# Attention parts at fixed places of each product pair, and the silus in another order, in a float32 encoder block on one core

## The chip, the cores and the metric

The kernel runs on one core of one Trainium2 chip. The metric is the device time of one execution in microseconds (us). Times of several runs are given by their median. One further execution was taken with the hardware profiler; durations of single instructions come from it. TensorE (PE) does the matrix products, VectorE (DVE) and ScalarE (ACT) the elementwise work, GpSimd (POOL) and SyncE (SP) issue most of the DMAs.

## The reference

One layer over 1024 tokens of width 1024 in float32, cut to what matters here:

```python
h = rmsnorm(x, norm_g)
q, k, v, za, u, vs, zs, gm = split(h @ w_in)
a   = window_sink_attention(rope(q), rope(k), v, sinks)     # 16 heads, 2 key heads, chunks of 64, window 192
a   = (a * silu(za)) @ w_att_out
sgo = chunked_spatial_gating(gelu(u), gelu(vs), ...)        # result s1 in the kernel
sgo = (sgo * silu(zs)) @ w_sg_out
ga, gs = split(sigmoid(gm + b_merge))
y   = ga * a + gs * sgo
out = rmsnorm(x + y @ w_o, final_g)
```

The attention subtracts the row's maximum (or the sink, if that is larger), takes exp, adds exp of the sink to the sum, and divides.

## The kernel before, in words

Every large product is done for a pair of 128-row blocks of the result at once, by a seven-product scheme of Strassen's kind on halves of the operands. Each factor is split into a rounded part (h) and a rest (l), and each of the seven products is 12 matmuls of 128 x 512. `gemm_pair` (L347) runs them in the order b11, t1, t2, b21, t3, b22, t4, named after the form of the activations that they use. They gather in three PSUM tiles: `acc` in a bank of ps_mm (b11, t2, t3, t4), `t5` in one of ps_o (t1, b22) and `t2` in one of ps_o (b21). There are two banks of each name. ACT copies x11, x22 and x12 out behind b11, t1 and t2 (L356, L360, L363), DVE adds the rest behind b21, t3 and b22 (L368, L373, L377). Each finished quarter (i, half) is handed to `finish`, in the order (0,0), (1,1), (0,1), (1,0); the last comes straight from `acc`, with sign -1. Behind each product `gemm_pair` calls a `hook`, so there are seven hooks in a pair, and `split_next` (L205) splits weights of the next pair there (L152, L153).

The stretch that the change touches has twelve pairs. Four compute zs: `zs_pair` with m = 0, 2, 4, 6. Then come four that compute the gate gs and four that compute ga; these only store their quarters. In this text they are called Z0 to Z3, S0 to S3 and A0 to A3. `zs_pair` (L1014) keeps the four quarters until the pair's products are written, then has a silu for each (L1032) and a multiplication by a block of s1 (L1042), and stores the product. The blocks of s1 are fetched into tiles "rot" in Z0 (five buffers, shared with the rotation of queries) and "g" in Z1 to Z3 (two buffers; two fetches are issued at the third hook, the others when a buffer is free). `after` ties instructions of one engine to an order without a semaphore: the first silu comes behind the last exp that stands ahead of it in the program, and the other silus behind the first. Silu and Exp need different tables of ACT, which are loaded on each change.

The attention has 32 steps n, each a group of heads on 128 tokens, and is written as a generator, `attention` (L1173), that yields after each part. A step has three parts:

- s(n), `softmax_stage` (L1060): scores into the two banks of ps_sc (L1075), row minima on DVE (L1083, L1084), four exps on ACT (L1086), one for the sink (L1096), sum and reciprocal on DVE (L1097, L1099), scaling on DVE (L1105) and ACT (L1107). It is followed by the query loads of step n + 2 on SP (L1000).
- w(n), `weight_stage` (L1110): eight transposes into two banks of ps_tp (L1127, L1138), split on ACT and DVE (L152, L153, tiles pT and pTb).
- v(n), `value_stage` (L1143): six matmuls into a bank of ps_o (L1160), copied by ACT (L1166) and added by DVE (L1167) into aT; every second one stores aT on POOL (L1169) and has the next value loads issued on SP (L981 to L991).

The generator's order is s0, s1, w0, s2, and then w(n-2), s(n), v(n-3) over and over: 96 parts. `part_of_attention` (L1213) is the hook of Z1 to A3 and decides how many parts run at a hook: one at each in Z1, Z2 and Z3, and 75/56 on average in the other eight pairs, by a running credit. Seven and 75/7 do not divide by three, so each pair finds the cycle at another place. From Z2 on each hook also calls `part_of_early` (L436), which at every second call has POOL issue one step of sums of later weights.

What is written first has priority, but the order of an engine's instructions in the trace is not that of the program: the framework's scheduler fills an engine with what its own model holds to be ready.

Of the kernel before, what the change touches and what calls it, by code (L numbers as in the profile page):

```python
# [33 lines left out]
KC = D // P  # L34
# [18 lines left out]
def hybrid_tile(  # L53
# [101 lines left out]
    def after(second, first):  # L155

        tc.add_manual_dep(
            second.ins,
            first.ins.name,
            mybir.DependencyInfo(mybir.DependencyClass.NoSync, mybir.DependencyReason.DATA),  # L160
            reason="order",
        )
# [184 lines left out]
    def gemm_pair(b, finish, hook=lambda: None, second="o"):  # L347

        n = done[0]
        done[0] += 1
        acc = bank("mm")[:]
        x11, x12, x22 = xtile(), xtile(), xtile()
        product(acc, ready[n, 0], b["b11"], True)
        pace[0] = nc.scalar.copy(x11[:], acc)  # L356
        hook()
        t5 = bank("o")[:]
        product(t5, ready[n, 2], b["t1"], True)
        pace[0] = nc.scalar.mul(x22[:], t5, -1.0)  # L360
        hook()
        product(acc, ready[n, 3], b["t2"], False)
        pace[0] = nc.scalar.copy(x12[:], acc)  # L363
        split_next()
        hook()
        t2 = bank(second)[:]
        product(t2, ready[n, 1], b["b21"], True)
        term[0] = nc.vector.tensor_add(x11[:], x11[:], t2)  # L368
        finish(0, 0, x11, x11[:], 1.0)
        split_next()  # L370
        hook()
        product(acc, ready[n, 4], b["t3"], False)
        term[0] = nc.vector.tensor_sub(x22[:], x22[:], acc)  # L373
        finish(1, 1, x22, x22[:], 1.0)
        hook()
        product(t5, ready[n, 5], b["b22"], False)
        term[0] = nc.vector.tensor_add(x12[:], x12[:], t5)  # L377
        finish(0, 1, x12, x12[:], 1.0)
        split_next()
        hook()  # L380
        product(acc, ready[n, 6], b["t4"], False)
        finish(1, 0, xtile(), acc, -1.0)
        split_next()
        hook()
# [51 lines left out]
    def part_of_early(every=2):  # L436
        hooks[0] += 1
        if early and hooks[0] % every == 0:
            early.pop(0)()
# [4 lines left out]
    def put(dst, m, half, src, queue=nc.sync):  # L444
        queue.dma_start(place(dst, m, half), src)

    def get(src, m, half, bufs, tag="g"):
        g = mtile([P, HALF], F32, tag, bufs, pool)
        copy_to(g[:], place(src, m, half))
        return g  # L450
# [319 lines left out]
    def hook():  # L770
        for _ in range(2):
            if late:
                late.pop(0)()
# [240 lines left out]
    def zs_pair(m, hook, *place, ahead_by=0):  # L1014
        quarters, fetched, hooked = [], [], [0]

        def fetch(i, half):
            fetched.append(get(s1_dr, m + i, half, *place))

        def step():  # L1020
            hook()
            hooked[0] += 1
            if hooked[0] == ahead_by:
                for at in ((1, 0), (0, 0)):
                    fetch(*at)

        gemm_pair(hb, lambda *quarter: quarters.append(quarter), step)

        quarters = quarters[-1:] + quarters[:-1]
        first = None  # L1030
        for i, half, q, src, sign in quarters:
            silu = nc.scalar.activation(q[:], src, AF.Silu, scale=sign)  # L1032
            first = first or silu
            if silu is not first:
                after(silu, first)
            elif exps:
                after(silu, exps[-1])
        for i, half, q, src, sign in quarters:
            if not fetched:
                fetch(i, half)  # L1040
            g = fetched.pop(0)
            nc.vector.tensor_mul(q[:], q[:], g[:])  # L1042
            put(s_dr, m + i, half, q[:])

    steps_of_q += [rotate(1, 1), first_loads()]
    zs_pair(0, part_of_q, 5, "rot")
    stage.close()

# [124 lines left out]
    def attention():  # L1173

        held, weights = [], []
        tiles = [step[:2] for step in steps[::2]]

        def weigh(n):  # L1180
            weights.append(weight_stage(*steps[n], held.pop(0)))

        def value(n):
            value_stage(*steps[n], weights.pop(0))
            if n % 2 and n + 3 < len(steps):
                value_loads(*tiles[n // 2 + 2])

        for n, step in enumerate(steps):
            if n >= 2:
                weigh(n - 2)  # L1190
                yield
            held.append(softmax_stage(*step, qT.pop(0)))
            if n + 2 < len(steps):
                qT.append(query_stage(*steps[n + 2]))
            if n in (0, 2):
                value_loads(*tiles[n // 2])
            yield
            if n >= 3:
                value(n - 3)
                yield  # L1200
        last = len(steps)
        for n in (last - 2, last - 1):
            weigh(n)
            yield
            value(n - 1)
            yield
        value(last - 1)
        yield

    parts = attention()  # L1210
    credit = [0.0]

    def part_of_attention(m=KC):  # L1213
        if m > 2:
            part_of_early()
        credit[0] += 1 if m < KC else 75 / 56
        while credit[0] >= 1:
            credit[0] -= 1
            next(parts, None)

    for m in range(2, KC, 2):
        zs_pair(m, lambda: part_of_attention(m), 2, ahead_by=3)
    for dst in (gs_dr, ga_dr):
        for m in range(0, KC, 2):
            gemm_pair(hb, rest(dst, m), part_of_attention)
# [438 lines left out]
```

## Time and profile before

| | |
|---|---|
| median of 3 runs | 939.69 us (939.38, 939.69, 942.12) |
| profiled execution, its own time | 939.98 us |
| span from its first to its last instruction | 938.1 us |
| mean granted clock of TensorE | 0.996 |
| Z1 to A3, about | 322 to 622 us of the span |

A page of the profile gives the busy time and instructions of each engine, then groups of instructions, with what ended the idle time ahead of them ("<-"). L338 is the one line that issues the matmuls of all seven products; the tile names tell them apart. In the timeline a row is `start, duration, engine, line, operation, out<-in, shapes, count [idle before <-releaser]`. A matmul's duration is modelled and overlaps the next one, so the distance of starts is the better measure. The table by windows has the busy time of PE, PEld (weight loads), DVE, ACT and POOL in each stretch, then granted clock, DMA share and GB/s. The waits are listed as waiting line, releasing line: us in total, times, longest.

### The profile page before, as it was taken

The numbers are of one execution on the slowest core, as the hardware profiler recorded it, in microseconds if no ns is written. First come the engines' busy times: TensorE is split into PE (matmuls) and PEld (weight loads), VectorE is DVE, ScalarE is ACT, GpSimd is POOL, SyncE is SP. The second block draws the span as 40 slices with busy tenths as digits, with TensorE's granted clock in tenths as the row PEclk, the third lists the DMA queues.
The fourth block names the chain that finished last, engine by engine and source line by source line (L and its number), as shares of the span: only waits on it lengthen the run. The fifth ranks groups of instructions, "written<-read, shape, count | busy, mean of one in ns | idle before, by whom it ended". The sixth has DMA issues, their size and how long they took to land.

```text
span 938.1 us, 13590 instructions
## 1 busy us (share of the span) xinstructions
PE 917.9 (98%) x4525; PEld 768.9 (82%) x4525; DVE 677.0 (72%) x1218; ACT 531.6 (57%) x1057; POOL 123.0 (13%) x199
## 2 busy tenths in 40 slices
PE   7999999999999999999999999999999999999996
PEld 6898888888888878888888888888887887888885
DVE  6755577665668678787878877756499489668996
ACT  7864343333445468777656676744475565457443
POOL 1211212221000001111111111101110011210012
PEclk9999999999999999999999999999999999999999
DMA  7343767888686778777777778859668754998622
GB/s 282 120 149 119 216 212 200 173 164 178 214 271 232 244 217 212 214 201 206 202 209 249 236 177 239 229 178 379 209 203 308 282 197 157 294 298 297 203 112 114
DMA packets 131301, 201.60 MB, mean 215 GB/s; under 512 B 12320, under 2 KB 64032, under 8 KB 131232
## 3 DMA queue, kind: packets, MB, share of 16 engines
q1 hardware_dynamic: 113616, 152.23, 49.0%
q0 software_dynamic: 17472, 48.24, 21.3%
q8 instruction: 36, 0.59, 0.3%
q14 instruction: 33, 0.27, 0.1%
q10 hardware_dynamic: 144, 0.26, 0.1%
HBM read 144.59 MB, written 85.46 MB: 245 GB/s over the span
## 4 chain that ended last, share of the span: by engine, by line
PE 75%; DVE 11%; ACT 5%; DMA 4%; issue 4%; SPq 1%; DVEq 0%; ACTq 0%
PE ps_mm L338 29%; PE ps_o L338 22%; PE ps_mm L624 6%; PE ps_tp L338 2%; PE ps_o L575 2%; PE ps_sc L1075 2%; PE ps_o L1160 2%; PE ps_sc L338 2%; DVE wl L153 2%; PE ps_tp L818 2%; ACT pr L1086 1%; DVE bq L182 1%; PE ps_tp L624 1%; PE ps_sc L624 1%; PE ps_o L624 1%
## 5 line engine op out<-in xcount | busy, mean ns | idle before, releaser
L152 ACT CAST wh<-s 128x1024 fp32r<-128x1024 f32 (+1 forms) x76 | 76.0, 1003 | 92.1 <-PE ps_mm L338 43.9
L153 DVE TENSOR_TENSOR wl<-wr,wh 128x1024 fp32r<-128x1024 f32 (+1 forms) x78 | 73.7, 947 | 53.6 <-ACT wh L152 52.9
L152 ACT CAST wh<-wr 128x1024 fp32r<-128x1024 f32 (+1 forms) x78 | 64.4, 829 | 80.4 <-PE ps_mm L338 33.7
L153 DVE TENSOR_TENSOR wl<-s,wh 128x1024 fp32r<-128x1024 f32 (+1 forms) x76 | 88.5, 1165 | 17.8 <-ACT wh L152 16.2
L1086 ACT ACTIVATE pr<-ps_sc,sm 128x192 f32<-128x192 f32 (+2 forms) x128 | 51.1, 410 | 35.6 <-DVE sm L1084 27.8
L338 PE MATMUL ps_o<-T_t1h,wh 128*128 128x512 f32 x144 | 57.1, 397 | 0.3 <-ACT wh L152 0.2
L338 PE MATMUL ps_o<-T_b22h,wh 128*128 128x512 f32 x144 | 57.2, 397 | 0.0
L338 PE MATMUL ps_o<-T_t1h,wl 128*128 128x512 f32 x144 | 56.3, 391 | 0.1
L338 PE MATMUL ps_o<-T_b22h,wl 128*128 128x512 f32 x144 | 56.2, 390 | 0.0
L338 PE MATMUL ps_o<-T_b22l,wh 128*128 128x512 f32 x144 | 56.1, 390 | 0.0
L338 PE MATMUL ps_o<-T_t1l,wh 128*128 128x512 f32 x144 | 56.1, 390 | 0.0
L338 PE MATMUL ps_mm<-T_b11h,wl 128*128 128x512 f32 x136 | 53.3, 392 | 2.0 <-DVE wl L153 2.0
L338 PE MATMUL ps_mm<-T_t3h,wh 128*128 128x512 f32 x136 | 54.1, 398 | 0.0
L338 PE MATMUL ps_mm<-T_t4h,wh 128*128 128x512 f32 x136 | 53.9, 396 | 0.0
L338 PE MATMUL ps_mm<-T_b11h,wh 128*128 128x512 f32 x136 | 53.7, 395 | 0.0
L338 PE MATMUL ps_mm<-T_t2h,wh 128*128 128x512 f32 x136 | 53.3, 392 | 0.2 <-ACT x L356 0.2
L338 PE MATMUL ps_mm<-T_t3l,wh 128*128 128x512 f32 x136 | 53.2, 391 | 0.0
L338 PE MATMUL ps_mm<-T_t3h,wl 128*128 128x512 f32 x136 | 53.2, 391 | 0.0
L338 PE MATMUL ps_mm<-T_t4h,wl 128*128 128x512 f32 x136 | 53.2, 391 | 0.0
L338 PE MATMUL ps_mm<-T_t2h,wl 128*128 128x512 f32 x136 | 53.0, 390 | 0.0
L338 PE MATMUL ps_mm<-T_b11l,wh 128*128 128x512 f32 x136 | 53.0, 390 | 0.0
L338 PE MATMUL ps_mm<-T_t4l,wh 128*128 128x512 f32 x136 | 53.0, 390 | 0.0
(374 smaller groups left out, 2474.8 us busy)
## 6 DMA issues: line engine op xcount, KB each, us to landing
wr<-in_w_dram SPq DMA_DIRECT2D x82, 256.0 KB
sums<-in_w_dram POOLq DMA_DIRECT2D x20, 512.0 KB, 5.3
s<-sums SPq DMA_DIRECT2D x20, 512.0 KB
s_dr<-x SPq DMA_DIRECT2D x32, 256.0 KB
q_hl<-qhl SPq DMA_DIRECT2D x16, 512.0 KB
q<-q_hl SPq DMA_DIRECT2D x64, 128.0 KB
wr<-in_w_dram SPq DMA_DIRECT2D x14, 512.0 KB
y_dr<-x POOLq DMA_DIRECT2D x28, 256.0 KB, 6.0
```

Of the source, the lines that this page charges most:

```text
L152: nc.scalar.copy(hi, src)
L153: return nc.vector.tensor_sub(lo, src, hi.bitcast(F32))
L182: op(dst[:, i : i + 2, :], a[:, i : i + 2, :], c[:, i : i + 2, :])
L338: nc.tensor.matmul(acc, lt, rt, start=fresh and k == 0 and n == 0, stop=k == 3 and n == 2, skip_group_check=True,)
L575: nc.tensor.matmul(acc[:, 0:256], lt[:, k, :], rt[:, k * 256 : (k + 1) * 256], start=j == 0 and k == 0 and n == 0, stop=j == 1 and k == 3 ...
L624: mm = nc.tensor.matmul(acc, lt, rt, start=k == 0 and n == 0, stop=k == KC - 1 and n == 2)
L818: nc.tensor.matmul(pm[:, t * P : (t + 1) * P], xh[:, half * 4 + t, g * P : (g + 1) * P], bias[-1][1][:, g % 4, :], start=True, stop=True,)
L1075: nc.tensor.matmul(sc[:, i, k0:], q_of[:, c, i * P : (i + 1) * P], kt[:, f, k0:], start=f == 0, stop=f == 1,)
L1086: nc.scalar.activation(pr[:, c, i, 0 : hi - lo], sc[:, i, lo:hi], AF.Exp, bias=nmax[:, c, i : i + 1], scale=-1.0, accum_out=sums[:, c, i : ...
L1160: nc.tensor.matmul(po[:, cs], lt, rt, start=n == 0, stop=n == len(terms) - 1)
```

## The change

Two things change, both in the stretch Z0 to A3.

The hook no longer counts credit. Z1 has one part at each of its seven hooks, as before. From Z2 on every pair has nine parts, (1, 2, 1, 1, 1, 2, 1) at its seven hooks. As nine divides by three, each pair meets the same cycle: w behind b11, s and v behind t1, w behind t2, s behind b21, v behind t3, w and s behind b22, v behind t4. In all there are 7 + 10 x 9 = 97 places for the 96 parts. `part_of_early` is called at the same hooks as before.

The silus, the multiplications and the stores of a zs pair follow the order of the quarters, (0,0), (1,1), (0,1), (1,0), where before the last was put first. The two fetches at the third hook are those of (0,0) and (1,1), where before they were (1,0) and (0,0).

Parts at the seven hooks, worked out from the two versions of the code:

| pair | before | after |
|---|---|---|
| Z1 | s0, s1, w0, s2, w1, s3, v0 | the same |
| Z2 | w2, s4, v1, w3, s5, v2, w4 | w2, s4+v1, w3, s5, v2, w4+s6, v3 |
| Z3 | s6, v3, w5, s7, v4, w6, s8 | w5, s7+v4, w6, s8, v5, w7+s9, v6 |
| S0 | v5, w7, s9+v6, w8, s10, v7+w9, s11 | w8, s10+v7, w9, s11, v8, w10+s12, v9 |
| S1 | v8, w10+s12, v9, w11, s13+v10, w12, s14 | the same cycle, three steps on, and so in all that follow |
| S2 | v11+w13, s15, v12, w14+s16, v13, w15, s17+v14 | |
| S3 | w16, s18, v15+w17, s19, v16, w18+s20, v17 | |
| A0 | w19, s21+v18, w20, s22, v19+w21, s23, v20 | |
| A1 | w22+s24, v21, w23, s25+v22, w24, s26, v23+w25 | |
| A2 | s27, v24, w26+s28, v25, w27, s29+v26, w28 | |
| A3 | s30, v27+w29, s31, v28, w30+v29, w31, v30 | w29, s31+v28, w30, v29, w31, v30+v31, none |

```diff
@@ zs_pair
             if hooked[0] == ahead_by:
-                for at in ((1, 0), (0, 0)):
+                for at in ((0, 0), (1, 1)):
                     fetch(*at)
 
         gemm_pair(hb, lambda *quarter: quarters.append(quarter), step)
 
-        quarters = quarters[-1:] + quarters[:-1]
         first = None
         for i, half, q, src, sign in quarters:
             silu = nc.scalar.activation(q[:], src, AF.Silu, scale=sign)
@@ after attention()
     parts = attention()
-    credit = [0.0]
-
-    def part_of_attention(m=KC):
-        if m > 2:
+    of_pair = [0]
+
+    PARTS = (1, 1, 2, 1, 1, 1, 2)
+
+    def part_of_attention(first=False):
+        if not first:
             part_of_early()
-        credit[0] += 1 if m < KC else 75 / 56
-        while credit[0] >= 1:
-            credit[0] -= 1
+        of_pair[0] += 1
+        for _ in range(1 if first else PARTS[of_pair[0] % 7]):
             next(parts, None)
 
     for m in range(2, KC, 2):
-        zs_pair(m, lambda: part_of_attention(m), 2, ahead_by=3)
+        zs_pair(m, lambda: part_of_attention(m == 2), 2, ahead_by=3)
```

## The prediction

> **What bounds the kernel now.** I read the page first, then the waits of TensorE between 300 and 625 us (all pairs that the change touches), the windows pair by pair, and the timeline of the places named there. Pairs are called Z0 to Z3, S0 to S3 and A0 to A3; parts s, w and v are softmax, weights and values of one attention step.
>
> ```profile
> span 938.1 us, 13590 instructions
> PE 917.9 (98%) x4525; PEld 768.9 (82%) x4525; DVE 677.0 (72%) x1218; ACT 531.6 (57%) x1057; POOL 123.0 (13%) x199
> ...
> PE ps_o L338 <- DVE aT L1167: 2.1, 2, 1.2
> PE ps_sc L1075 <- ACT pr L1086: 1.7, 1, 1.7
> PE ps_tp L1127 <- ACT pr L1107: 0.5, 1, 0.5
> ...
> PEld ps_o L338 <- DVE aT L1167: 4.0, 5, 1.4
> ```
>
> TensorE is busy 98% of the span, so an order of parts can only move the few microseconds in which it waits. Two kinds of wait are left here: products into bank ps_o that wait for DVE to empty it of a value result (L1167), and a start-up stall at the first softmaxes (L1086, L1107).
>
> ```profile
> 336.00:338.00 2.00, 0.54 (x3) 0.11 (x1) 2.00 (x8) 1.82 (x5) 0.00 (x0) 1.00 0.93 305
> ...
> 340.00:342.00 2.00, 1.50 (x7) 0.85 (x7) 1.76 (x9) 1.37 (x7) 0.00 (x0) 0.54 0.89 270
> 342.00:344.00 2.00, 2.00 (x9) 1.77 (x9) 0.48 (x3) 1.91 (x9) 0.00 (x0) 0.61 0.86 228
> ...
> 351.00:376.00 25.00, 24.83 (x132) 20.74 (x131) 21.02 (x47) 20.56 (x52) 3.30 (x4) 1.00 0.83 217
> 376.00:402.60 26.60, 25.37 (x137) 21.62 (x136) 20.79 (x44) 19.74 (x46) 4.17 (x5) 1.00 0.82 222
> 402.60:430.10 27.50, 27.49 (x152) 23.53 (x151) 23.12 (x51) 21.91 (x57) 4.15 (x5) 1.00 0.80 221
> 430.10:457.80 27.70, 27.55 (x153) 23.20 (x152) 21.46 (x49) 18.06 (x50) 4.14 (x5) 1.00 0.76 198
> 457.80:486.50 28.70, 27.81 (x159) 23.99 (x158) 21.28 (x49) 19.00 (x52) 3.87 (x5) 1.00 0.68 194
> ```
>
> Columns: stretch, then busy us of PE, PEld, DVE, ACT and POOL, granted clock, DMA share, GB/s. The rows from 351 on are pairs Z2, Z3, S0, S1 and S2. The first three rows are the start-up: PE stands 1.46 us in 336 to 338, and then the granted clock is 0.54 and 0.61 for four microseconds, which costs 2 x 0.46 + 2 x 0.39 = 1.7 us more. In the pairs PE stands 0.17, 1.23, 0.01, 0.15 and 0.89 us.
>
> **The stalls at b21.** A value part fills the second ps_o bank, and b21 needs it. Four places show it:
>
> ```profile
> 386.56 0.85 PE L1075 MATMUL ps_sc<-k,q 128*128 128x256 f32 x5
> 388.64 0.50 PE L338 MATMUL ps_o<-T_b21h,wh 128*128 128x512 f32 x1 [1.23 <-DVE aT L1167]
> ...
> 446.77 0.39 PE L338 MATMUL ps_o<-T_b22l,wh 128*128 128x512 f32 x1
> 447.29 0.50 PE L338 MATMUL ps_o<-T_b21h,wh 128*128 128x512 f32 x1
> ...
> 471.32 0.40 PE L338 MATMUL ps_mm<-T_t3l,wh 128*128 128x512 f32 x1
> 472.61 0.50 PE L338 MATMUL ps_o<-T_b21h,wh 128*128 128x512 f32 x1 [0.89 <-DVE aT L1167]
> ...
> 499.55 0.39 PE L338 MATMUL ps_mm<-T_t3h,wh 128*128 128x512 f32 x1
> 499.78 0.39 PE L338 MATMUL ps_mm<-T_t3l,wh 128*128 128x512 f32 x1
> 500.26 0.50 PE L338 MATMUL ps_o<-T_b21h,wh 128*128 128x512 f32 x1
> ```
>
> Undisturbed 512-wide matmuls start 0.23 apart (499.55 and 499.78). So b21 came late by 447.29 - 446.77 - 0.23 = 0.29 in S1, 472.61 - 471.32 - 0.23 = 1.06 in S2 and 0.25 in S3: together 1.60. In Z3 the idle time is 1.23; a 256-wide row whose next starts 0.14 on (0.85 less 0.28 over four) hides another 0.15, so 1.4. In S1, S2 and S3 a value stands behind t2, directly ahead of b21. In Z3 it does not: v3 stands behind t1. There DVE came late for another reason.
>
> ```profile
> 386.00 0.69 DVE L1042 TENSOR_TENSOR x<-x,g 128x512 f32<-128x512 f32 x1 [0.91 <-DMA g<-s_dr]
> ...
> 387.89 0.69 DVE L1167 TENSOR_TENSOR aT<-aT,ps_o 64x512 f32<-64x512 f32 x1
> ```
>
> DVE stood 0.91 us at the third gate multiplication of Z2, waiting for a fetch of g, and the addition that empties ps_o was queued behind it.
>
> **The change, part by part.**
>
> *Values behind products 2, 5 and 7.* Removed: every value between t2 and b21. If b21 of S1, S2 and S3 then starts on time, that is -1.60; the ends are 0 (the bank is late from the earlier place too) and, with Z3, the 4.0 that weight loads waited. What the new place gives is already in the trace: A0 before runs w19, s21+v18, w20, s22, v19+w21, s23, v20, the locked order but for one part, and there
>
> ```profile
> 549.57 0.69 DVE L1167 TENSOR_TENSOR aT<-aT,ps_o 64x512 f32<-64x512 f32 x1 [0.95 <-ACT aT L1166]
> ...
> 550.31 0.60 PE L1138 MATMUL ps_tp<-ident,pr 128*64 128x128 f32 x4
> 550.67 0.48 PE L338 MATMUL ps_o<-T_b21h,wh 128*128 128x512 f32 x1
> ```
>
> the bank was empty at 549.57 + 0.69 = 550.26 and b21 followed its transposes at 550.67. The cover, t2 and the four-and-four transposes, is just enough: 0.41 us to spare. Where DVE is later than that, b21 stalls by the rest. I take -1.60 for S1 to S3.
>
> *The same place in Z2, Z3 and S0.* Here the gate multiplications of the pair before lie on DVE, and their third and fourth wait for fetches that can only be issued when the first two have freed their buffers. Z3 has this order already and keeps its 1.4: 0. S0 had v6 behind t2 and 0.01 idle; now v7 stands behind t1 with the multiplications ahead of it: between 0 and +1.4, and I take +0.5, nearer to zero because the silus of Z3 will follow a softmax behind b22 and not one behind t4, so they begin earlier than now. Z2: the same ends; its 0.17 of idle came with v1 already done behind t1's scores, so 0.
>
> *Two more parts in Z2 and Z3 (nine, not seven), 3 to 4 fewer over the other eight.* The sum of parts is 96 in both, so PE work moves and costs nothing. What moves into Z2 is one s and one v:
>
> ```profile
> L1086 ACT ACTIVATE pr<-ps_sc,sm 128x192 f32<-128x192 f32 x88 | 36.0, 420 | 27.8 <-DVE sm L1084 20.1 <-PE ps_o L338 3.9 <-PE ps_o L1160 3.5
> L1083 DVE TENSOR_REDUCE sm<-ps_sc 128x2 f32<-128x384 f32 x44 | 23.1, 552 | 3.1 <-PE ps_sc L1075 2.9
> ...
> L1107 ACT ACTIVATE pr<-pr,sm 128x192 f32<-128x192 f32 x44 | 17.7, 449 | 2.8 <-DVE sm L1099 2.6
> L1167 DVE TENSOR_TENSOR aT<-aT,ps_o 64x512 f32<-64x512 f32 x25 | 17.1, 685 | 7.8 <-ACT aT L1166 7.5
> ...
> L1166 ACT COPY aT<-ps_o 64x512 f32<-64x512 f32 x25 | 14.5, 581 | 6.0 <-PE ps_o L1160 5.5
> ...
> L1105 DVE TENSOR_SCALAR pr<-pr,sm 128x192 f32<-128x192 f32 x44 | 12.1, 317 | 0.7
> ...
> L1084 DVE TENSOR_TENSOR sm<-sm,nsink_sb 128x2 f32<-128x2 f32 x48 | 7.0, 155 | 0.3
> ```
>
> On DVE an s is 2 x 0.552 + 2 x 0.317 + five small ones at about 0.155 = 2.5, a v 0.69: +3.2. On ACT 4 x 0.42 + 2 x 0.449 and a small one, 2.8, and 0.58: +3.4. PE gets 14 matmuls at 0.14 or less, under +2.0. Z2 had DVE 21.0 and ACT 20.6 busy in 25 us; it will have 24.2 and 24.0 in about 26.8, 90% each, where the fullest pair now (S0, 23.1 of 27.5) has 84%. If DVE keeps the 4.0 us in which it stands now, it needs 28.2: +1.4. If it fills them, 0. S0 at 84% lost 0.01, so I take +0.5. Z3 gets a w and a v from a lower start (20.8 in 26.6): 0. Their DMAs go with them: one query load (two issues on SP) and one set of value loads, about half a megabyte against 217 GB/s x 25 us = 5.4 MB, on engines at 0.83; and one store on POOL, which stands waiting for values anyway:
>
> ```profile
> POOL at_dr L1169 <- DVE aT L1167: 133.3, 14, 20.5
> ```
>
> *The silus in the order of their quarters.* Now the quarter out of t4 goes first, so no silu can start before t4 ends; then the first silu needs only its own sum and the last exp ordered ahead of it. Four silus and one load of their table per pair stay:
>
> ```profile
> L1032 ACT ACTIVATE x<-x x12: 615/619/627, 325.3 to 409.6; 128x512 f32<-128x512 f32 x12
> L1032 ACT ACT_TABLE_LOAD  x4: 1283/1283/1283, 323.6 to 406.0; - x4
> ```
>
>  In Z1, Z2 and Z3 the last exp binds, behind b22: the gain is part of the terms above. The bank ps_mm of t4 comes free three silus later, and the second ps_mm bank, which the next pair uses, hides that. In Z0 there is no exp, so the silus move up into ACT's free time, and with them the first multiplication. But the start-up hangs on something else:
>
> ```profile
> 326.72 1.47 SPq L197 DMA_DIRECT2D rot<-s_dr  x3
> ...
> 331.49 0.69 DVE L1042 TENSOR_TENSOR x<-x,rot 128x512 f32<-128x512 f32 x1 [5.32 <-ACT wh L152]
> ```
>
> Three of Z0's fetches are issued at 326.72, after SP has worked off eight stores of rotated queries and two weight loads, and DVE stands 5.3 us for the first of them; the first softmax is queued behind these multiplications on DVE. (The row names an ACT cast that ended just then; the landing at 331.4 fits the fetch.) The change leaves the SP queue ahead of these fetches as it is. So the start-up stays: 0. Its ends: if the fetches went out earlier, all of 1.7 + 0.5 + 1.7 = 3.9 could go; if the table load and one silu hold up the casts of rotated queries, and the stores with them, 1.28 + 0.62 = 1.9 comes on top.
>
> A rule stands beside that price. The Trainium skill (TensorE: Matmul & The Clock Gate, Part 1) has the clock halved after an idle window of about 3.4 us. The trace halves it after less, 1.46 us of idle in a sparse stretch, and did not after the 1.23 us in Z3 (granted 1.00). By the page alone a shortened start-up stall would already be free of the halving; by the trace it takes more than a small shortening, and the sum keeps it.
>
> **The sum.** -1.60 (S1 to S3) + 0.5 (S0) + 0.5 (Z2) = -0.6. The profiled execution took 939.98 us, of which 938.1 are span; it becomes 939.4. The median of the three runs shown lies 0.3 lower, so I predict 939.1.
>
> **Rivals.**
>
> *The locked order also clears Z3 and what is left in the S pairs.* All four b21 stalls go, 1.6 + 1.4, S0 and Z2 cost nothing, and the 0.5 at L1107 in the start-up goes with earlier multiplications: -3.5, 936.2. For: in A0 and its like PE hardly stands. Against: those pairs have no gate multiplications on DVE.
>
> *The gate fetches decide, three times.* In Z2, Z3 and S0 the value behind t1 waits behind multiplications that wait for g, as Z3's does now: 2 x 1.4 more. Z2's DVE adds its full 1.4, Z3's with w and v 0.5, and S1 to S3 give back only 1.6: +3.1, 942.8. It decides from the point at which the addition on DVE is over 0.41 us later than in A0. For: the 0.91 us wait at 386.00. Against: at other places the list put t3 or b22 ahead of b21 (446.77), which hides such a wait.
>
> *The start-up gets worse.* Silus early on ACT delay the casts of rotated queries by a table load and a silu, SP's chain and the first softmax with them: +1.9, and a second stretch at half clock +1.7, less 0.6: +3.0, 942.7.
>
> *Nothing moves.* The order of PE is not the program's (b22 ahead of b21 above), so values may end up where they were: 0, 939.7; this lies inside the forecast's own range.
>
> **How the numbers follow.** What a measurement can tell here is about 0.3%, 2.8 us: the three runs spread from 939.38 to 942.12. The forecast, with "nothing moves", has 0.46 and its own range is 937.0 to 941.2; the first rival 0.26, the second 0.19, the third 0.09. Faster by over 0.3% (under 936.9): most of the first rival and a little of the forecast, 0.27. Slower (over 942.5): most of the second and third and a little of the forecast, 0.31. The rest, 0.42, is within. The range takes in the rivals' times: 935.3 to 943.6.
>
> **What would show it.** Right: waits of TensorE for DVE at L1167 fall from 2.1 to about 1.2 to 1.5 and what is left lies in Z2, Z3 or S0; b21 of S1 to S3 follows its transposes by 0.2 to 0.4; the start-up stall before 344 with its half clock is still there; four silu table loads. Wrong: L1167 waits in every pair (the cover of 0.41 is too thin), DVE at 95% in Z2 with PE standing, or a start-up without the low clock.

## The result and the profile after

The changed kernel takes 936.77 us (median of 5 runs, 936.11 to 937.03) against 940.37 for the kernel before on the same chip (939.38 to 942.12): ratio 0.9964, 95% interval 0.995 to 0.9978. On a second chip, measured later with 12 runs, it took 938.79 against 940.87: 0.9976 [0.9962, 0.999]. So it is faster, by 3.6 and 2.1 us on medians; whether by more than the 0.3% named in the prediction is not settled, as the two figures lie on either side of it. The forecast, 939.1, had the sign, but its 0.6 us is a sixth of the 3.6 here and a quarter to a third of the 2.1 there; 936.77 lies just below its own range (937.0 to 941.2) and inside the wide one. The first rival, 936.2, comes closest.

The profiled execution took 936.77 us (before 939.98). Lines from the silus on are one lower than before: the addition that empties ps_o is L1166 (was L1167), the gate multiplication L1041, the scores L1074, the exps L1085. Page, then all waits of TensorE over 0.1 us between 300 and 625 us:

```profile
span 934.7 us, 13576 instructions
PE 916.9 (98%) x4525; PEld 769.1 (82%) x4525; DVE 677.6 (72%) x1218; ACT 530.9 (57%) x1057; POOL 123.0 (13%) x199
...
PE ps_sc L1074 <- ACT pr L1085: 1.9, 1, 1.9
PE ps_tp L1126 <- ACT pr L1106: 0.6, 1, 0.6
PE ps_mm L338 <- ACT x L356: 0.2, 1, 0.2
```

The same work (the counts of PE, DVE, ACT and POOL are those of before), and no wait for the aT addition at all, where there were 2.1 us on PE and 4.0 on PEld. The start-up stall is left, and 0.2 us ahead of t2 in Z2.

How late TensorE was, stage by stage, follows from the distances between starts: for each shape of matmul the median distance to the next start is taken as usual, and what lies above it is summed. How finely shapes are told apart and how small an excess still counts moves a whole column: with one median per shape and every excess counted, S1 to A3 has 6.5 before and 3.7 changed, where the table has 4.1 and 1.3. The difference between rows is the same 2.8, and only differences are used here. The windows are those of the clock, so pairs shift in them by up to 3 us. Each row is one execution, and the halved clock that it happened to have is in it, 1.7 us for each 3.4 us of it: in the start-up of all rows but silus alone, the two with two fetches and the two late starts without POOL (twice as much in parts alone, in value behind t2 and in late start with fetches on POOL), and in Z2 and Z3 of silus alone, fetches on POOL (1.7 each) and lock from S0 (3.4). All profiled executions are in one table, as the experiments below are read by it:

| us above the usual distances | start-up 300–348 | Z2, Z3 348–403 | S0 403–430 | S1 to A3 430–625 | 700 to end |
|---|---|---|---|---|---|
| before | 4.7 | 2.5 | 0.8 | 4.1 | 3.6 |
| changed | 5.5 | 1.6 | 1.0 | 1.3 | 3.1 |
| changed, second chip | 5.2 | 3.2 | 1.2 | 1.3 | 3.2 |
| parts alone | 6.5 | 1.6 | 1.2 | 1.6 | 3.4 |
| silus alone | 3.1 | 5.5 | 0.9 | 4.7 | 3.2 |
| value behind t2 | 6.4 | 3.6 | 1.1 | 4.7 | 4.2 |
| lock from S0 | 4.6 | 7.9 | 1.2 | 1.5 | 3.3 |
| before, two fetches | 4.0 | 1.6 | 0.6 | 4.0 | 3.2 |
| changed, two fetches | 3.7 | 1.4 | 0.8 | 1.6 | 3.2 |
| fetches on POOL | 7.4 | 4.8 | 0.1 | 1.7 | 3.2 |
| late start | 2.8 | 3.0 | 0.4 | 1.6 | 3.3 |
| late start, second chip | 3.3 | 4.2 | 1.0 | 1.7 | 3.5 |
| late start, fetches on POOL | 8.8 | 4.0 | 1.2 | 1.6 | 3.7 |

From before to changed: +0.8 - 0.9 + 0.2 - 2.8 - 0.5 = -3.2 us, against 3.4 of span. The last term lies behind the stretch that the change touches; its cause was not looked for.

In S1 to A3, b21 stands directly behind the transposes in every pair. Timeline of the changed kernel, TensorE in S1 and S2, and DVE in S1:

```profile
442.14 0.68 DVE L1166 TENSOR_TENSOR aT<-aT,ps_o 64x512 f32<-64x512 f32 x1 [0.37 <-ACT aT L1165]
...
444.50 0.60 PE L1137 MATMUL ps_tp<-ident,pr 128*64 128x128 f32 x4
444.86 0.48 PE L338 MATMUL ps_o<-T_b21h,wh 128*128 128x512 f32 x1
...
471.33 0.60 PE L1137 MATMUL ps_tp<-ident,pr 128*64 128x128 f32 x4
471.69 0.48 PE L338 MATMUL ps_o<-T_b21h,wh 128*128 128x512 f32 x1
```

The bank is empty at 442.14 + 0.68 = 442.82, and b21 starts 2.04 us later: not a thin cover here. In Z3 it is thin, but it holds, and the reason was not in the prediction:

```profile
388.27 0.69 DVE L1041 TENSOR_TENSOR x<-x,g 128x512 f32<-128x512 f32 x1
...
389.02 0.67 DVE L1166 TENSOR_TENSOR aT<-aT,ps_o 64x512 f32<-64x512 f32 x1
390.67 0.69 DVE L1041 TENSOR_TENSOR x<-x,g 128x512 f32<-128x512 f32 x1 [0.98 <-DMA g<-s_dr]
...
389.67 0.60 PE L1137 MATMUL ps_tp<-ident,pr 128*64 128x128 f32 x4
390.02 0.48 PE L338 MATMUL ps_o<-T_b21h,wh 128*128 128x512 f32 x1
```

DVE still stands for a fetch of g (0.98), but at the fourth multiplication, and the aT addition now lies ahead of it. The bank is empty at 389.69, 0.33 before b21.

In Z2 and S0 it is different again. There the multiplication that waits for g does lie ahead of the aT addition, but the scheduler put seven matmuls of b22 and two of t3 between the transposes and b21. DVE and TensorE in S0:

```profile
417.99 0.69 DVE L1041 TENSOR_TENSOR x<-x,g 128x512 f32<-128x512 f32 x1 [1.57 <-DMA g<-s_dr]
...
419.90 0.69 DVE L1166 TENSOR_TENSOR aT<-aT,ps_o 64x512 f32<-64x512 f32 x1
...
420.73 0.39 PE L338 MATMUL ps_mm<-T_t3l,wh 128*128 128x512 f32 x1
420.96 0.39 PE L338 MATMUL ps_o<-T_b21h,wh 128*128 128x512 f32 x1
```

The bank is empty at 420.59, and TensorE has the other products to run until 420.96.

The start-up is what it was. SP, DVE and the windows (PE, PEld, DVE, ACT, POOL, granted clock, DMA share, GB/s):

```profile
319.25 5.20 SPq L897 DMA_DIRECT2D q_hl<-qhl  x8
324.49 2.38 SPq L197 DMA_DIRECT2D wr<-in_w_dram  x2
...
327.39 1.45 SPq L197 DMA_DIRECT2D rot<-s_dr  x3
...
331.70 0.69 DVE L1041 TENSOR_TENSOR x<-x,rot 128x512 f32<-128x512 f32 x1 [5.95 <-DMA rot<-s_dr]
...
336.00:338.00 2.00, 0.74 (x4) 0.28 (x2) 2.00 (x8) 1.36 (x2) 0.00 (x0) 1.00 0.70 219
...
340.00:342.00 2.00, 1.36 (x6) 0.84 (x6) 1.97 (x10) 0.91 (x5) 0.00 (x0) 0.81 0.92 284
342.00:344.00 2.00, 2.00 (x10) 1.77 (x8) 0.60 (x4) 2.00 (x12) 0.00 (x0) 0.50 0.94 245
344.00:346.00 2.00, 2.00 (x11) 1.76 (x11) 1.56 (x5) 0.36 (x2) 0.00 (x0) 0.83 0.64 137
```

The fetches of Z0 leave SP 0.7 us later than before (327.39, 326.72), DVE waits 5.95 us for the first, and the clock is halved again (granted 0.81, 0.50 and 0.83).

### The profile page after: what moved, and what is told of

Same layout as the page of the kernel before. It is cut to its first block, busy times and chain, and to the rows that moved or that the text cites. A ratio compares the mean times of both kernels' runs of the same rounds, so it can differ in the third digit from the quotient of the medians.

```text
span 934.7 us, 13576 instructions
## 1 busy us (share of the span) xinstructions
PE 916.9 (98%) x4525; PEld 769.1 (82%) x4525; DVE 677.6 (72%) x1218; ACT 530.9 (57%) x1057; POOL 123.0 (13%) x199
## 4 chain that ended last, share of the span: by engine, by line
PE 82%; DVE 8%; DMA 3%; ACT 3%; issue 2%; SPq 1%; DVEq 0%; ACTq 0%
PE ps_mm L338 33%; PE ps_o L338 24%; PE ps_mm L624 6%; PE ps_sc L1074 3%; PE ps_sc L338 2%; PE ps_tp L338 2%; PE ps_o L1159 2%; PE ps_o L575 2%; PE ps_tp L818 2%; DVE wl L153 1%; PE ps_tp L1126 1%; PE ps_tp L1137 1%; PE ps_tp L624 1%; PE ps_sc L624 1%; PE ps_o L624 1%
## 5 line engine op out<-in xcount | busy, mean ns | idle before, releaser
L1085 ACT ACTIVATE pr<-ps_sc,sm 128x192 f32<-128x192 f32 (+2 forms) x128 | 50.9, 409 | 18.7 <-PE ps_o L1159 14.2
L338 PE MATMUL ps_mm<-T_t2l,wh 128*128 128x512 f32 x136 | 53.0, 390 | 0.0
```

The costliest lines, as they stand in the source:

```text
L338: nc.tensor.matmul(acc, lt, rt, start=fresh and k == 0 and n == 0, stop=k == 3 and n == 2, skip_group_check=True,)
L1085: nc.scalar.activation(pr[:, c, i, 0 : hi - lo], sc[:, i, lo:hi], AF.Exp, bias=nmax[:, c, i : i + 1], scale=-1.0, accum_out=sums[:, c, i : ...
```

## The experiments

Theory A: the places of the parts bring the gain, in S1 to A3 by a value that no longer stands ahead of b21, in Z3 by a value that comes to DVE ahead of the waiting multiplication. Rivals: the order of the silus and their fetches brings it; or a regular cycle, wherever the value stands; or the two more parts in Z2 and Z3. In the kernels below L1166 and L1169 too are the aT addition, as lines shift.

**Parts alone** (order of silus and fetches as before):

```
-                for at in ((0, 0), (1, 1)):
+                for at in ((1, 0), (0, 0)):
...
+        quarters = quarters[-1:] + quarters[:-1]
```

> The nine parts at fixed places, with the silus, multiplications and fetches of Z0 to Z3 in the old order (quarter of t4 first). Theory A, the place of the values is all: as the changed kernel, ratio to before 0.9964 (0.995 to 0.998), no wait of TensorE for the addition L1167, Z3 included. Theory B, Z3's 1.4 us went because the silus start earlier: TensorE waits about 1.2 us at b21 of Z3 again, ratio 0.998.

936.91 us, ratio 0.9958 [0.9944, 0.9973]: all of the gain. TensorE's order is the changed kernel's, and Z3 and S1 to A3 are as free (table). The order of the silus adds nothing to these places.

**Silus alone** (credit as before, silus and fetches in the new order):

```
-    PARTS = (1, 1, 2, 1, 1, 1, 2)
+    credit = [0.0]
...
+        credit[0] += 1 if m < KC else 75 / 56
+        while credit[0] >= 1:
+            credit[0] -= 1
```

> The silus in the order of their quarters, with the old running credit of parts. Theory A: as before, ratio 1.000 (0.9985 to 1.0015), the waits of TensorE for L1167 still near 2 us and in Z3 and S2. Theory B: the wait in Z3 goes, about 1.2 us less, the one in S2 stays; ratio 0.9985.

943.92 us, 1.003 [1.0017, 1.0043]: slower, which neither theory had. In its profile the loss is in Z3. Timeline of this kernel, SP, DVE and TensorE:

```profile
376.09 1.24 SPq L197 DMA_DIRECT2D g<-s_dr  x1
...
380.92 0.45 SPq L197 DMA_DIRECT2D g<-s_dr  x1
...
379.21 1.31 DVE L1041 TENSOR_TENSOR x<-x,g 128x512 f32<-128x512 f32 x2
...
386.55 0.69 DVE L1041 TENSOR_TENSOR x<-x,g 128x512 f32<-128x512 f32 x1 [4.71 <-DMA g<-s_dr]
...
388.15 0.69 DVE L1166 TENSOR_TENSOR aT<-aT,ps_o 64x512 f32<-64x512 f32 x1
...
388.89 0.50 PE L338 MATMUL ps_o<-T_b21h,wh 128*128 128x512 f32 x1 [2.61 <-DVE aT L1166]
```

The third fetch of Z2 goes out at 376.09. The fourth needs the buffer of the second multiplication, which runs only at 379.21, together with the third; it goes out at 380.92, 4.8 us after the third, and the fourth multiplication starts 5.6 us after that. DVE stands 4.71 us for it, with the aT addition behind it, and b21 stands 2.61; the clock is halved behind this stall, and that makes 1.7 of the 5.5 us in the table. In S1 to A3 this kernel has 4.7 us, near the 4.1 of the kernel before.

**Value behind t2** (nine parts in the same regular way, but w, s, v + w, s, v, w + s, v):

```
-    PARTS = (1, 1, 2, 1, 1, 1, 2)
+    PARTS = (1, 1, 1, 2, 1, 1, 2)
```

> As the changed kernel, still nine parts a pair at fixed places, but the first value of each pair is moved from behind t1 to behind t2 (w, s, v+w, s, v, w+s, v at the seven hooks). Theory A, the place decides: the waits at b21 come back in most of the ten pairs, 0.3 to 1.4 us each, so 3 to 10 us over the changed kernel, 940 to 947. Rival C, it is the regular cycle of nine that counts, whatever the places, and the scheduler puts another product ahead of b21: within 1 us of the changed kernel, 936 to 938.

941.21 us, 1.0004 [0.999, 1.0019]: the gain is gone. A regular cycle is not what pays. TensorE's waits between 300 and 625, and b21 of Z3, S0 and S2:

```profile
PE ps_o L338 <- DVE aT L1166: 2.7, 3, 1.4
...
399.02 0.50 PE L338 MATMUL ps_o<-T_b21h,wh 128*128 128x512 f32 x1 [1.41 <-DVE aT L1166]
...
426.74 0.50 PE L338 MATMUL ps_o<-T_b21h,wh 128*128 128x512 f32 x1 [0.22 <-DVE aT L1166]
...
477.85 0.50 PE L338 MATMUL ps_o<-T_b21h,wh 128*128 128x512 f32 x1 [1.07 <-DVE aT L1166]
```

Not in every pair, however: in S1, in S3 and from there on the scheduler put five to eight matmuls of t3 ahead of b21, which hides most of the wait. In Z3 and S0 it put all of t3 and eight or nine matmuls of b22 there, and b21 is late even so.

**Lock from S0** (one part at each hook of Z1 to Z3 as before, then the locked cycle; silus new):

```
-        for _ in range(1 if first else PARTS[of_pair[0] % 7]):
+        for _ in range(1 if of_pair[0] < 22 else 2 if of_pair[0] == 22 else PARTS[of_pair[0] % 7]):
```

> Nine at fixed places only from S0 on: Z1, Z2 and Z3 have one part at each hook as in the kernel before, S0 has ten (v5+w7 at its first hook), the last two parts run behind A3; silus as in the changed kernel. Theory A: S1 to S3 run without a wait at b21, 1.6 us gained, Z3 (v3 behind t1, fetches of g ahead of it) waits again 1.2 to 2.8 us: 938 to 939.5. Rival H, the two extra parts in Z2 and Z3 cost something that is saved here: 936 or less.

941.7 us, 0.9996 [0.9986, 1.0006]: over both expectations. S1 to A3 are clean, 1.5; Z3 is the worst of all. SP, DVE, TensorE and windows:

```profile
382.26 0.44 SPq L197 DMA_DIRECT2D g<-s_dr  x1
...
389.27 0.69 DVE L1041 TENSOR_TENSOR x<-x,g 128x512 f32<-128x512 f32 x1 [6.09 <-DMA g<-s_dr]
...
390.86 0.69 DVE L1166 TENSOR_TENSOR aT<-aT,ps_o 64x512 f32<-64x512 f32 x1
...
391.61 0.79 PE L338 MATMUL ps_o<-T_b21h,wh 128*128 128x512 f32 x1 [4.02 <-DVE aT L1166]
...
390.00:392.00 2.00, 0.39 (x1) 0.40 (x2) 1.87 (x6) 1.66 (x4) 0.15 (x1) 0.56 0.52 183
392.00:394.00 2.00, 2.00 (x6) 1.52 (x6) 1.97 (x5) 1.09 (x3) 2.00 (x4) 0.50 0.72 186
```

With the new silu order and the old places of parts, b21 of Z3 waits for the fourth block of s1. How long depends on when it comes: 5.6 us after its issue above, 7.0 here (382.26 to 389.27), and the stall grows alike, from 2.61 to 4.02. The changed kernel itself has 4.7 us for this fetch in one execution and 6.6 in the other, so how much of the longer stall belongs to the silu order is not shown by single profiles; that the order costs in this place is shown by the medians of silus alone. The places of the parts in Z2 and Z3 keep the wait off b21: it does not stand in either profile of the changed kernel. The two more parts there are no cost that shows: with them Z2 and Z3 lose 1.6 and 3.2, without them 7.9, of which 3.4 is half clock.

**Two fetches, before and changed** (the third and fourth multiplication of Z1 to Z3 reuse the blocks of the first two):

```
             g = fetched.pop(0)
+            if ahead_by:
+                fetched.append(g)
             nc.vector.tensor_mul(q[:], q[:], g[:])
```

> The kernel before, but Z1 to Z3 fetch only two of their four blocks of s1 and multiply the third and fourth quarter by the first two again (six of the twelve g fetches and their factors are left out). Theory A2, Z3's stall is DVE standing for a g fetch ahead of the addition L1167: it falls from 1.2 us to under 0.3, those of S1 to S3 stay; ratio to before 0.9985. Rival G, the bank is late for another reason (place behind t1): 1.2 us stay, ratio 1.000.

> The changed kernel with the same cut (two of four blocks of s1 fetched in Z1 to Z3, the others left out and the first two used again). If g fetches still cost the changed kernel anything, it shows here: Z2 and S0 lose about 1 us each by start distances, of which up to half could go, 935.8 to 936.8; if ACT's silus and table loads are the cause, nothing changes, 936.5 to 937.

Before with two fetches: 939.53 us, 0.9978 [0.9967, 0.9988]; changed with two fetches: 934.85, 0.9927 [0.9913, 0.9941]. TensorE at b21 of Z3 and S2 in the first:

```profile
387.10 0.50 PE L338 MATMUL ps_o<-T_b21h,wh 128*128 128x512 f32 x1 [0.43 <-DVE aT L1169]
...
470.43 0.50 PE L338 MATMUL ps_o<-T_b21h,wh 128*128 128x512 f32 x1 [0.88 <-DVE aT L1169]
```

In Z3 the wait falls from 1.23 to 0.43, in S2 it stays (0.89, 0.88): two stalls of the same instruction with two causes, for the most part a DMA in Z3 and the place of the value in S2. The wait in Z3 was expected under 0.3. The changed kernel with two fetches is faster than either expectation; by the ratios the fetches left out still cost it 0.4% (0.9927 against 0.9964, intervals apart). Where, its one profile does not settle. The start-up goes from 5.5 to 3.7, but 1.7 of that is the half clock that this execution did not have, and silus alone and the late start, with all fetches, lack it too. Z2 and Z3 go to 1.4, from 1.6 in the first profile of the changed kernel and 3.2 in the second.

**Fetches on POOL.** What is left of the start-up: Z0's fetches, queued on SP behind stores, are issued by POOL.

```
-            fetched.append(get(s1_dr, m + i, half, *place))
+            if m:
+                fetched.append(get(s1_dr, m + i, half, *place))
+                return
+            g = mtile([P, HALF], F32, place[1], place[0], pool)
+            nc.gpsimd.dma_start(g[:], s1_dr[(m + i) * P : (m + i + 1) * P, half_of(half)])
+            fetched.append(g)
```

> As the changed kernel, but the four fetches of s1 blocks in Z0 are issued by POOL instead of SP, so that they do not stand behind the stores of rotated queries and weight loads. Start-up theory (DVE stands behind the late fetches): the multiplications of Z0 are done before 329, the first exp comes some 4 us sooner, the 2 us stall near 336 and the half clock are gone: 3.5 to 5 us faster than the changed kernel, 932 to 933.5. Rival D (ACT stands for the store of s_dr until 330.7 and the exps come behind that): 1 to 2.5 us, 934.5 to 936. Rival E (the stall has another cause): 936 to 937.5.

940.67 us, 1.0001 [0.9985, 1.0016]: a miss, 0.4% over the changed kernel by the ratios. Timeline, DVE, ACT and TensorE:

```profile
328.63 0.69 DVE L1046 TENSOR_TENSOR x<-x,rot 128x512 f32<-128x512 f32 x1 [0.29 <-DMA rot<-s_dr]
...
333.01 1.28 ACT L1090 ACT_TABLE_LOAD   x1 [6.39 <-DMA s_dr<-x]
...
335.06 1.81 PE L1079 MATMUL ps_sc<-k,q 128*128 128x128 f32 x8 [3.77 <-ACT pr L1090]
```

Z0's multiplications are done by 329.3 instead of 335.4, and the first exps come 3.6 us earlier (the table load at 333.01, not 336.63), yet TensorE stands 3.77 us for them and not 1.94. The scheduler had put the second scores in the middle of t2, and TensorE comes to them at 331.29, not 336.74: 5.45 us earlier, more than the softmax gained. The five matmuls of t2 left and the products behind them come after the wait.

**Late start.** The other way round: Z1 has no part at its first three hooks, so the first softmax is asked for later.

```
-        for _ in range(1 if first else PARTS[of_pair[0] % 7]):
+        for _ in range(int(of_pair[0] > 3) if first else PARTS[of_pair[0] % 7]):
```

> As the changed kernel, but Z1 has its first part at the fourth hook: s0, s1, w0, s2 behind b21, t3, b22, t4 and nothing before; every later pair keeps nine parts at the same places, three parts behind, and the last two run behind A3. Start-up theory: the first exps cannot run before about 336.6 whatever the order, so TensorE loses time only because the second scores stand in its queue at 336; with t3 ahead of them the 2 us stall and the half clock after it go: 2 to 5 us faster than the changed kernel, 932 to 935. Rival F: the parts pressed together at the end of Z1 make the same stall there, 936 to 938.

937.01 us, 0.9955 [0.9941, 0.9969], within the 936 to 938 of rival F. Both versions were then run side by side on the second chip, with a third that has the fetches on POOL as well:

> The changed kernel as it is, on one chip with the late start. On the chips so far it took 0.9964 of the kernel before [0.995, 0.9978]; 0.995 to 0.998 is expected here, with the stall at the first softmaxes of about 5 us of start distances between 336 and 348 us, partly at half clock.

> The changed kernel with Z1's first three hooks without a part, beside the changed kernel itself on the same chip. If the stall at the first softmaxes is a cost of its own, this is 1 to 2 us faster than the changed kernel of the same call (its one profile had 1.2 us less of excess start distances up to 403 us, and no stretch at half clock). If the stall only moves to the parts that are then left for later, the two are within 0.7 us.

> Z0's four fetches of s1 issued on POOL and Z1's first three hooks without a part. Fetches on POOL alone had Z0's multiplications done 6 us earlier but let the second scores in ahead of a softmax that was still waiting for the stores of rotated queries. If that early place was what cost, the late start takes it away and the result is 1 us or more under the late start alone. If the fetches on POOL disturb another thing (the stall of 2.35 us in Z3, reductions of early weights on POOL), it is again at 3 to 4 us over the changed kernel.

Changed 0.9976 [0.9962, 0.999], late start 937.31 us and 0.9966 [0.9953, 0.9979], late start with fetches on POOL 940.02 us and 0.9997 [0.9983, 1.0011], 1.2 us over the changed kernel and so between its two expectations. The late start's profiles have the full clock throughout the start-up, 1.9 to 2.7 us less there (1.7 of it the half clock) and 1 to 1.4 more in Z2 and Z3. It is 1.5 us ahead of the changed kernel on medians, but the intervals overlap: better, if at all, by a tenth of a per cent. Its stall has moved rather than gone. TensorE in the late start, and in the one with POOL:

```profile
335.56 0.50 PE L338 MATMUL ps_mm<-T_t3h,wh 128*128 128x512 f32 x1 [1.29 <-ACT x L363]
```

```profile
337.47 0.50 PE L338 MATMUL ps_mm<-T_t3h,wh 128*128 128x512 f32 x1 [2.85 <-ACT x L363]
```

Now a product waits for the copy that frees a bank of ps_mm. Why fetches on POOL make that copy later still was not pursued.

The second profile of the changed kernel shows how near the edge the rest is:

```profile
392.46 0.69 DVE L1041 TENSOR_TENSOR x<-x,g 128x512 f32<-128x512 f32 x1 [2.91 <-DMA g<-s_dr]
...
399.76 1.23 DVE L153 TENSOR_TENSOR wl<-wr,wh 128x1024 fp32r<-128x1024 f32 x1
400.90 1.01 DVE L1082 TENSOR_REDUCE sm<-ps_sc 128x2 f32<-128x384 f32 x2
...
401.90 0.68 DVE L373 TENSOR_TENSOR x<-x,ps_mm 128x512 f32<-128x512 f32 x1
...
402.63 0.50 PE L338 MATMUL ps_mm<-T_t4h,wh 128*128 128x512 f32 x1 [1.05 <-DVE x L373]
```

The addition behind t3 of Z3 is queued behind a split and a reduction on DVE, and t4 stands 1.05 us. The first profile has no such wait. That is most of the 3.2 against 1.6 in Z2 and Z3. DVE's backlog goes back to the fourth fetch: it stood 2.91 us for it at 392.46, where the first profile has 0.98, and in the 9.45 us from 393.15 to 402.60 it stands only 0.66. So the gate fetch no longer holds b21 of Z3, but a late one can still cost a product behind it.

## Why the prediction was right or wrong

*-1.60 at b21 of S1 to S3: right as a mechanism, and too small.* The three b21 start on time in all of the profiles with the locked cycle. The whole stretch S1 to A3 gives 2.8, from 4.1 to 1.3: beside the 1.60 are smaller delays that the sum did not count: 0.19 ahead of t3 in S1 (442.69), 0.23 ahead of a value in A0 (555.81), and many of under 0.1. This part is settled: every kernel with the locked cycle has 1.3 to 1.7 in this stretch, the three with the credit have 4.0 to 4.7, and the cycle with the value behind t2 has 4.7.

*"Z3 has this order already and keeps its 1.4: 0". This is the step that failed most.* The order of parts around t1 is the same, but what was taken to follow from it depends on the order on DVE. ACT loads the table for Z2's silus at these times, in the kernel before and in the changed one:

```profile
377.85 1.28 ACT L1032 ACT_TABLE_LOAD   x1
```

```profile
381.70 1.28 ACT L1031 ACT_TABLE_LOAD   x1
```

The nine parts put s6 into Z2, ahead of its silus, where before it stood at the first hook of Z3; the silus are ordered behind its exps, the multiplications move back with them, and the list then has the aT addition ahead of the multiplication that waits for its fetch. So the term for Z3 should have been -1.4 at b21 and not 0. Z2 and Z3 together lose 1.6 and not 2.5 in the first profile; in the second the late fetch takes that back at t4 (3.2).

*+0.5 in S0 and +0.5 in Z2: wrong.* The windows of Z2, Z3 and S0 in the changed kernel, from the start of each pair's b11 to that of the next:

```profile
352.00:378.40 26.40, 26.16 (x145) 22.05 (x144) 22.25 (x50) 21.73 (x55) 3.33 (x4) 1.00 0.83 224
378.40:405.80 27.40, 27.40 (x153) 23.41 (x152) 23.26 (x52) 21.92 (x56) 4.95 (x6) 1.00 0.86 220
405.80:433.30 27.50, 27.37 (x151) 23.01 (x150) 23.14 (x53) 22.35 (x56) 3.34 (x4) 1.00 0.83 223
```

TensorE stands 0.24 us in Z2 and 0.13 in S0, where it stood 0.17 and 0.01. The danger seen for b21 was real: the multiplications did lie ahead of the addition, and DVE stood 1.3 us for g in Z2 and 1.6 in S0. What the sum missed is that the scheduler fills such a place with b22 and t3, as it had done before at 446.77. The load of DVE in Z2 was over-counted as well: 22.25 of 26.40 us and not 24.2 of 26.8, 84% and not 90%. About 1.2 us came into Z2 and not 3.2, and 2.5 into Z3, for which the prediction put the effect at 0. That sum took a pair's parts to run within the pair's products, and the scheduler moves work across the border.

*The silus at 0, the start-up at 0: right on the whole.* Silus alone cost +0.3%, and nothing of that shows once the parts are locked; the prediction had no term for it, and it expected Z3's silus to begin earlier with the change. They hardly do: their table load starts 3.3 us behind the start of S0 (409.09 and 405.83), where it was 3.4 (406.04 and 402.63). The SP chain ahead of Z0's fetches was read rightly, and so was the half clock that stays.

*The rivals.* The first (-3.5) came true in size, in part by luck: S1 to A3 gave 2.8 and not 1.6, Z2 and Z3 0.9 and not 1.4, and the start-up nothing. Its mechanism held with one exception: the wait at L1107 in the start-up is still there (0.5, now 0.6). Against it stood that pairs without gate multiplications prove nothing for Z3; that was a fair objection to its reason, and the silus-alone and lock-from-S0 kernels show that the danger is real. The second rival names that danger: a multiplication that waits for g ahead of the aT addition on DVE. It cost 2.6 us in one of those kernels and 4 in the other, and a half clock behind each. In the changed kernel it did not decide: in Z3 the addition went first, and in Z2 and S0, where it did not, other products stood ahead of b21. The fourth, nothing moves, fell with the clean b21.

Of its own list of signs, the start-up with its half clock and the clean b21 of S1 to S3 came true; the wait at L1167 was to fall to 1.2 to 1.5 and fell to 0.

## What to carry to other kernels

When parts of another stage are woven into products, fix them to places where the bank that they borrow is emptied before the next product that needs it: count the work between the two in the trace, and look for a pair that already has that order. Then read the order on the engine that empties the bank, since a stall of one product can have two causes: here one was the place of the part, the other an operation that waited for a DMA ahead of it in DVE's queue. Look also at what the scheduler puts ahead of that product, as this hid the same wait in two pairs. An order that is neutral in one schedule (the silus) cost 0.3% in another. A step moved up by a list scheduler can cost more than it gains: a softmax that was ready 3.6 us earlier left TensorE standing twice as long.

## What the runs showed of the hardware

The granted clock was halved for 3.4 us or for twice that wherever it was, but for the kernel's end. With the half clock at 0.5, the time at it is 2 x 2 x (1 - granted clock) summed over the two-microsecond rows: before, 4 x (0.46 + 0.39) = 3.4; changed, 4 x (0.19 + 0.50 + 0.17) = 3.4; lock from S0, where TensorE stood about 4 us, 0.56, 0.50, 0.50 and 0.73 in the rows from 390 to 398, 6.8. So one halving costs 1.7 us or 3.4. The Trainium skill (TensorE: Matmul & The Clock Gate, Part 1) describes a free-running window of about 3.4 us that is not aligned to the kernel. The traces agree with it.

The clock records of a trace give the start of each halving, and within an execution the starts lie whole multiples of 3.4133 us apart: 51.20 us in lock from S0 (339.05 and 390.25, 15 times) and 61.44 in fetches on POOL (335.76 and 397.20, 18 times). In the kernel before, 340.15 and the halving at the kernel's end, 934.07, are 593.92 apart, 174 times. Against the kernel's start this grid lies elsewhere in each: the first halving is at 340.15 before, 341.26 changed, 340.82 in parts alone. Which share of a window must be idle is not shown.

The same stall is not always followed by a halving. Both two-fetch kernels stood 2.0 and 2.1 us between 336 and 342 by their windows and kept the full clock; the kernel before stood 2.2 there and lost it. The late start stood 1.3 us in one piece, on the second chip 1.5, at full clock. This goes with much of what executions of one kernel differ by: of the kernel before on the second chip, the fastest of 29 executions took 937.91 us at a mean clock of 0.998 and the slowest 944.64 at 0.992, and the clock that is missing makes about 5.7 of these 6.7 us.

The multiplication that waited for a block of 128 x 512 could start 3.2 to 7.0 us after the fetch was issued, over all such waits in Z1 to Z3 of the profiles. For one and the same fetch of the changed kernel, Z2's fourth, it was 4.7 us in one execution (385.95 to 390.67) and 6.6 in the other (385.81 to 392.46). With so much between two fetches of the same size, no place in the order with less room than that is safe for one.
